# Attention with a bias on one core: late loads throttled by halves, new load times and due slots in the planner, 24 instead of 25 score tiles on VectorE

## The chip, the cores and the metric

The kernel runs on one core of a Trainium2 chip. The metric is the device time of one execution in microseconds. The profile shows one further execution, whose own time is given beside its span (first to last instruction).

## What is computed

```python
def reference(q, k, v, bias):            # q, k, v: (4, 8, 1024, 64) float32, bias: (1, 1, 1024, 1024)
    scale = 1.0 / np.sqrt(head_dim)
    scores = scale * np.matmul(q, k.transpose(0, 1, 3, 2)) + bias
    scores_max = np.max(scores, axis=-1, keepdims=True)
    attn = np.exp(scores - scores_max) / (np.sum(np.exp(scores - scores_max), axis=-1, keepdims=True) + 1e-8)
    return np.matmul(attn, v)
```

There are 32 heads of 1024 queries and 1024 keys, with 64 elements a head. The kernel leaves the maximum out and gets the sum of the exponentials from a column of ones beside V.

## The kernel before

**Slots.** The heads are taken as 16 pairs, and the queries of a head as 8 chunks of 128. One chunk of one head is a *slot*: a tile of 128 x 1024 scores. There are 256. The list `slots` holds them in order: two groups of pairs (7 and 9 pairs), and inside a group rounds that take several query chunks of each head in turn. Three places in PSUM (`places`, tile `pl`) hold the scores of three slots. The scores of a slot are made as a difference: the tile that the last slot left in its place is kept, and one product with doubled operands (`ko`/`qo` for an odd head, `ke`/`qe` for an even one) takes the last head's scores out and puts the new one's in. Only where a chain starts, the bias is written first, by a product with an identity (line 255).

**What happens to a slot.** TensorE fills the place (`fill`, line 258, eight matmuls). ScalarE then makes the exponentials of the whole tile in one instruction (`exp`, line 272) into one of 13 buffers `E`. For the slots in `PLAN`, VectorE makes them instead, in five steps (`d_steps`, lines 289, 294, 297, 300 and 305). TensorE multiplies the result with V and its column of ones (`av`, line 322, eight matmuls) into a bank `po` that takes six or seven slots. VectorE divides by the sums (`evac`, lines 350 and 352), and SyncE's queue stores the result.

**What comes before.** Of each pair, K and Q are loaded by GpSimd's DMA queue, which also turns float32 into bfloat16, into `land` tiles (`k16`, `q16`, five buffers each). TensorE transposes them in pieces (`transposes`, lines 195 and 199) into one of the two small PSUM buffers `xa` and `xb`, which the products with V share. VectorE copies them out to `ko` and `qo` (`copy_out`, lines 207 and 209). For the pairs from 7 on (`EARLY`), Q is then negated back into the tile that it was loaded into (`negate`, line 232), and SyncE's queue copies halves of `ko` and of the negated Q to `ke` and `qe` of this pair and of the next (`copy`, line 583). The loads of pairs 7 to 15 go in two halves each, one DMA a head: K and Q in `beside` (line 142), V straight into its place in `vall` (line 170).

**Who sets the order.** No loop runs over this. A planner in Python goes through the engines by estimated clocks (`t_pe`, `t_act`, `t_dve`, `t_pool`, `t_dma`) and writes out one program. Each engine works its instructions off in that order, and waits for what a tile's last user or writer has to do. The estimates decide only the order. The parts that matter here:

- `issue` (line 492) estimates when a load lands and holds loads back. The list `flight` holds each load's last element and its estimated landing. Before a load that would be too many, GpSimd copies one element of the load `depth` places back (`tick`, line 497), and so waits until that one has landed. `LATE` (3) is the depth for pairs 7 to 15, `DEEP` (4 and 5) that for the earlier loads.
- `COSTS` (2300 ns a load) is the estimated time of a late load, and `t_dma` the estimated end of the last one.
- `load` (line 503) issues K and Q of a pair as soon as the pair five back has freed its tiles, then queues V of the pair before; `next_v` issues V once its place in `vall` is free.
- `DUE` gives, for pairs 7 to 15, the slot by which a pair's transposes are due; a pair can be taken up to `AHEAD` (90) slots before. If it is due within 20 slots, its copies go first on VectorE.
- `PLAN` lists the slots whose exponentials VectorE makes.

The functions that the diff touches, and what calls them:

Of the kernel before, what the change touches and what calls it, by code (L numbers as in the profile page):

```python
# [16 lines left out]
def kernel(  # L17
# [79 lines left out]
    for g, n in enumerate(GROUPS):  # L97
        heads = list(range(2 * pr0, 2 * (pr0 + n)))
        rounds = []
        a = (len(heads) * 2 // 3 + 1) // 2 * 2  # L100
        tail = [(2, c, h, h == heads[a]) for c in (3, 4) for h in heads[a:]]
        assert len(tail) <= a
        middle = [[(0, 3, h, h == heads[0]), (1, 4, h, h == heads[0])] + tail[i:i + 1] for i, h in enumerate(heads[:a])]
        ends = [[[(x, c + x, h, h == heads[0] and (go or g == 0)) for x in range(3)] for h in heads]
                for go, c in enumerate((5, 0) if g % 2 else (0, 5))]
        rounds = ends[0] + middle + ends[1]
        first_pair.add(pr0)
        group_of[pr0] = g
# [14 lines left out]
    for s, x in enumerate(slots):  # L123
# [2 lines left out]


    dslots = set()
    PLAN = (42, 46, 54, 72, 74, 83, 90, 97, 107, 112, 135, 138, 151, 158, 161, 173, 180, 186, 194, 207, 213,
            217, 228, 238, 246)  # L130

    raws, lands, arrs = {}, {}, {}


    BESIDE, INPLACE = (0, 1), 7

    def beside(pr, x):

        raws[pr, x, 0] = t = land.tile([P, 2, NCH, D], BF, name="qk"[x] + "16").rearrange(
            "p t c d -> p (t c d)").rearrange("p (c t d) -> p c t d", t=2, d=D)  # L140
        for y in range(2):
            nc.gpsimd.dma_start(out=t[:, :, y, :], in_=(qf, kf)[x][pr][:, y].rearrange("p (c d) -> p c d", d=D))  # L142
        return t[:1, NCH - 1, 1, D - 1:]

    def load_k(pr):
        if pr >= EARLY and 1 in BESIDE:
            return beside(pr, 1)
        lands[pr, 1, 0] = t = land.tile([P, 2, NCH, D], BF, name="k16")
        nc.gpsimd.dma_start(out=t.rearrange("p t c d -> p t (c d)"), in_=kf[pr])
        return t[:1, 1, NCH - 1, D - 1:]  # L150

    def load_q(pr, cs):
        if pr >= EARLY and 0 in BESIDE:
            return beside(pr, 0)

        t = consts.tile([P, 2, NCH - C0, D], BF, name=f"qrest{pr}") if cs.start else land.tile([P, 2, NCH, D], BF, name="q16")
        lands[pr, 0, cs.start] = t
        to = t[:, :, :cs.stop - cs.start, :]
        nc.gpsimd.dma_start(out=to.rearrange("p t c d -> p t (c d)"),
                            in_=qf[pr][:, :, cs.start * D:cs.stop * D])  # L160
        return to[:1, 1, cs.stop - cs.start - 1, D - 1:]

    def load_b(c):
        nc.gpsimd.dma_start(out=braw[:, c, :], in_=bf_[:, c, :])
        return braw[:1, c, S - 1:]

    def load_v(pr):
        if pr >= INPLACE:
            for t in range(2):
                nc.gpsimd.dma_start(out=vall[:, (2 * pr + t) % VR, :, :D], in_=vf[pr][:, t])  # L170
            return vall[:1, (2 * pr + 1) % VR, NCH - 1, D - 1:D]
        lands[pr, "v"] = vland.tile([P, 2, NCH, D], BF, name="v16")
        nc.gpsimd.dma_start(out=lands[pr, "v"].rearrange("p t c d -> p t (c d)"),
                            in_=vf[pr].rearrange("p t c d -> p t (c d)"))
        return lands[pr, "v"][:1, 1, NCH - 1, D - 1:]

    def arrays(pr):
        if pr not in arrs:
# [176 lines left out]
    with tc.manual_schedule():  # L355
# [14 lines left out]

        nc.gpsimd.memset(qz[0][D:, :, :], 0.0)  # L371
        nc.gpsimd.memset(qs[D:, :, :], 0.0)  # L372
        for c in (1, 2):
            load_b(c)
        load_k(1)
        load_q(1, slice(0, C0))
        load_k(2)
        load_q(2, slice(0, NCH))
        load_v(0)
# [82 lines left out]
        free_lands, loads, loads_v = set(), list(range(EARLY, NP)), []  # L462
        sp_q, t_sp = [], T0
# [25 lines left out]
            while loads and loads[0] - LANDS in free_lands:  # L489
                load(loads.pop(0), t)  # L490

        def issue(at, cost, depth, load, pr, *a):

            nonlocal t_dma
            if 0 < depth <= len(flight):
                what, t = flight[-depth]
                nc.gpsimd.tensor_copy(tick[:], what)
                at = max(at, t + 100)
            two = pr >= EARLY and load in [load_q] * (0 in BESIDE) + [load_k] * (1 in BESIDE) or load is load_v and pr >= INPLACE
            at = pool(at, 1500 if two else 750)  # L500
            t_dma = max(t_dma + cost, at + 2200 + cost)
            flight.append((load(pr, *a), t_dma + 200))
            return t_dma + 200

        def load(pr, t):
            raw_at[pr, 1, 0] = issue(t, COSTS["k"], LATE, load_k, pr) + LATER
            raw_at[pr, 0, 0] = issue(t, COSTS["q"], LATE, load_q, pr, slice(0, NCH)) + LATER
            for p in [pr - 1] * (pr > EARLY) + [pr] * (pr + 1 == NP):
                loads_v.append(p)
            next_v(t)  # L510

        def next_v(t):

            while loads_v and not any(x[2] // 2 == loads_v[0] - VR // 2 and y not in av_done for y, x in enumerate(slots)):
                if loads_v[0] < INPLACE + VL and loads_v[0] - VL not in v_at:
                    break
                p = loads_v.pop(0)
                vland_at[p] = issue(t, COSTS["v"], LATE + (p > 12), load_v, p) + LATER
                move_v(p)

        def move_v(pr):
            if pr >= INPLACE:
                v_at[pr] = vland_at[pr] + 300
                return

            def run(t2):
                nc.vector.tensor_copy(vall[:, 2 * pr % VR:2 * pr % VR + 2, :, :D], lands[pr, "v"][:])
                v_at[pr] = t2 + 430 + L_DVE
                next_v(v_at[pr])
            dve_q.append((vland_at[pr] + VSLACK * (pr >= EARLY), 0.3, 430, run))  # L530

        def early(kind, pr):
            nonlocal t_dma
            late = kind + str(pr) in LATE_LOADS
            depth = DEEP[late]
            if kind == "k":
                raw_at[pr, 1, 0] = issue(0, E1, depth, load_k, pr) + SLACK
            elif kind == "q":
                cs = slice(0 if pr >= SPLIT else C0, NCH)
                raw_at[pr, 0, cs.start] = issue(0, E1 if pr >= SPLIT else E2, depth, load_q, pr, cs) + SLACK  # L540
                if late:
                    raw_at[pr, 0, cs.start] = LATE_LOADS["q%d" % pr]
            elif kind == "v":
                vland_at[pr] = issue(0, E1, depth, load_v, pr)
                if late:
                    vland_at[pr] = LATE_LOADS["v%d" % pr]
                move_v(pr)
            else:
                issue(0, E1, depth, load_b, pr)
                bias_at[pr] = LATE_LOADS["b%d" % pr]  # L550
            if late:
                t_dma = LATE_LOADS[kind + str(pr)] - 200
                flight[-1] = flight[-1][0], t_dma + 200

        def doubles(pr, which, c0, n, t2, urgent):
            if not which and pr >= EARLY:
# [63 lines left out]
        def sided(pr, which, c0):  # L620
            return SIDE <= pr < EARLY and c0 == 0
# [13 lines left out]
        def pe_cands():  # L635

            out = []
            for x in range(3):
# [4 lines left out]
                if r is not None and (before[s] is None or before[s] in used):  # L643
                    cost = FILL + BIAS * bool(slots[s][3] and s > 1)

                    def do(t, s=s, x=x, cost=cost):
                        nonlocal next_fill
                        fill(s)
                        filled[s] = t + cost + L_FILL
                        queue[x].pop(0)  # L650
                        next_fill = min([y[0] for y in queue.values() if y], default=NS)
                        if s in PLAN:
                            dslots.add(s)
                            avq.remove(s)
                            start_d(s)
                        else:
                            acts.append(s)
# [47 lines left out]
            if pieces:  # L705
# [5 lines left out]
                if (raw is not None and next_fill >= need - AHEAD and (ring < 0 or last_slot[ring] < next_fill)  # L711
                        and (lag < 7 or need - next_fill < 6)):
                    f, tag = min((x_free[y], y) for y in x_free)
                    r = max(f, raw)
                    cost = n * TR + SWITCH * (which not in BESIDE if pr >= EARLY else not sided(pr, which, c0))
# [205 lines left out]
```

## Time and profile before

| | |
|---|---|
| time, three runs | 230.83 us median (230.78 to 232.82) |
| the profiled execution | 232.22 us, span 230.4 us, granted clock 0.996 |
| busy: TensorE, ScalarE, VectorE, GpSimd | 219.2, 216.8, 204.0, 82.2 us |
| DMA moved | 29.74 MB, 129 GB/s on average |
| GpSimd's queue (loads) | 62880 packets, 14.06 MB |
| SyncE's and ScalarE's queue (copies, stores, first loads) | 28080 packets, 14.43 MB |

The profile gives busy time, idle time and its releaser for each group of instructions; the columns read "busy us, mean ns of one | idle us before it, and who ended that". Matmuls are pipelined, and their ends are modelled, so neighbouring rows overlap: the pace is read from start to start. A releaser "issue" means that the engine waited for nothing that the profile shows.

### The profile page before, as it was taken

To read this page: it belongs to the slowest core of one execution; us is meant where nothing else is said; L and a number is where in the kernel's file an instruction comes from. 1 tells how busy PE (TensorE), PEld (TensorE's weight loads), DVE (VectorE), ACT (ScalarE), POOL (GpSimd) and SP (SyncE) were. 2 spreads that over 40 slices of the span, in tenths; PEclk is the share of its full clock that TensorE was granted. 3 is DMA by queue.
4 is the path that set the end of the run, shared out by engine and by line. 5 is a ranking of instruction groups with operands and counts; after the bars stand their busy time and mean duration, and the time that the engine had idled before them with its cause. 6 is when DMAs were issued, how large, how long until landed. Compare 5 with 4: busy or idle time off the path is not lost.

```text
span 230.4 us, 10433 instructions
## 1 busy us (share of the span) xinstructions
PE 219.2 (95%) x4535; PEld 208.9 (91%) x4535; DVE 204.0 (89%) x304; ACT 216.8 (94%) x236; POOL 82.2 (36%) x133
## 2 busy tenths in 40 slices
PE   7899999999999999779999899999999999999993
PEld 2779989999999999779999899998999998999992
DVE  3487878679989999879999899999999999999994
ACT  4699999999999999789999899999999999999993
POOL 8826454599668696586246000000000000000000
PEclk9999999999999999999999999999999999999998
DMA  6999999999999999999979975102122111211313
GB/s 206 195 205 215 226 221 207 185 169 152 197 171 159 134 145 175 195 188 145 146 159 163 192 165 135 50 0 54 42 47 69 38 29 32 68 43 43 83 29 82
DMA packets 91437, 29.74 MB, mean 129 GB/s; under 512 B 74560, under 2 KB 87744, under 8 KB 91392
## 3 DMA queue, kind: packets, MB, share of 16 engines
q0 software_dynamic: 62880, 14.06, 67.7%
q1 hardware_dynamic: 28080, 14.43, 26.2%
q8 instruction: 35, 0.57, 1.1%
q10 hardware_dynamic: 432, 0.59, 1.0%
q14 instruction: 10, 0.08, 0.1%
HBM read 29.36 MB, written 8.39 MB: 164 GB/s over the span
## 4 chain that ended last, share of the span: by engine, by line
PE 59%; ACT 19%; issue 9%; DVE 6%; DMA 3%; POOL 1%; SPq 1%; POOLq 0%; ACTq 0%
PE pl L258 34%; ACT E L272 19%; PE po L322 18%; PE px L195 4%; DMA braw<-in_bias_dram 3%; PE pl L255 2%; DVE dy L289 2%; PE px L199 1%; DVE ob L352 1%; DMA out_dram<-ob 1%; DVE df L297 1%; SPq L757 1%; POOL qz L371 0%; POOL qs L372 0%; DVE ke L218 0%
## 5 line engine op out<-in xcount | busy, mean ns | idle before, releaser
L272 ACT ACTIVATE E<-pl 128x1024 bf16<-128x1024 f32 (+1 forms) x232 | 213.6, 1089 | 5.6 <-PE pl L258 5.5
L322 PE MATMUL po<-vall,E 128*128 128x65 bf16 x1848 | 87.5, 194 | 2.0 <-issue 1.2
L258 PE MATMUL pl<-qo,ko 128*128 128x128 bf16 x1024 | 76.5, 219 | 2.5 <-issue 1.5
L322 PEld LDWEIGHTS <-E 128*128 128x128 bf16 x1848 | 74.5, 98 | 2.9 <-issue 1.3
L258 PEld LDWEIGHTS <-ko 128*128 128x128 bf16 x1160 | 69.8, 98 | 5.2 <-issue 2.7
L258 PE MATMUL pl<-qe,ke 128*128 128x128 bf16 x888 | 65.9, 219 | 0.8 <-DVE dy L289 0.4
L258 PEld LDWEIGHTS <-ke 128*128 128x128 bf16 x888 | 53.2, 98 | 2.5 <-issue 1.0
L289 DVE TENSOR_SCALAR dy<-pl 128x1024 int32<-128x1024 f32 x25 | 30.5, 1219 | 3.2 <-PE pl L258 3.0
L305 DVE SCALAR_TENSOR_TENSOR de<-dy,df 128x1024 uint16<-128x1024 int32 x25 | 30.5, 1218 | 0.5 <-PE po L322 0.5
L297 DVE SCALAR_TENSOR_TENSOR df<-df 128x1024 f32<-128x1024 f32 x25 | 30.5, 1219 | 0.1
L300 DVE SCALAR_TENSOR_TENSOR df<-df 128x1024 f32<-128x1024 f32 x25 | 30.4, 1217 | 0.1
L352 DVE TENSOR_TENSOR ob<-po,rs 128x448 f32<-128x448 f32 (+5 forms) x41 | 23.5, 572 | 1.4
L142 POOL DMA_DIRECT2D q<-in_q_dram x18 | 15.9, 886 | 8.8 <-DVE ob L352 7.5
L294 DVE TENSOR_SCALAR df<-dy 128x1024 f32<-128x1024 uint16 x25 | 17.4, 701 | 0.1
L142 POOL DMA_DIRECT2D k<-in_k_dram x18 | 15.9, 888 | 2.9 <-PE px L195 2.0
L170 POOL DMA_DIRECT2D vall<-in_v_dram x18 | 15.8, 884 | 1.0 <-issue 0.9
L209 DVE TENSOR_SCALAR qo<-px,sgn 128x1024 bf16<-128x1024 bf16 (+2 forms) x18 | 12.3, 683 | 1.5 <-PE px L199 1.0
L207 DVE COPY ko<-px 128x1024 bf16<-128x1024 bf16 (+1 forms) x16 | 10.7, 669 | 3.2 <-PE px L199 2.6
L255 PE MATMUL pl<-ident,braw 128*128 128x128 bf16 x136 | 11.4, 227 | 0.2 <-DMA braw<-in_bias_dram 0.2
L350 DVE RECIPROCAL rs<-po 128x7 f32<-128x7 f32 (+5 forms) x42 | 8.1, 194 | 3.5 <-PE po L322 3.1
L322 PE MATMUL po<-vall,de 128*128 128x65 bf16 x200 | 10.5, 194 | 0.2 <-DVE ob L352 0.2
L255 PEld LDWEIGHTS <-braw 128*128 128x128 bf16 x136 | 10.0, 149 | 0.4 <-DMA braw<-in_bias_dram 0.3
(63 smaller groups left out, 124.3 us busy)
## 6 DMA issues: line engine op xcount, KB each, us to landing
out_dram<-ob SPq DMA_DIRECT2D x69, 64.0 KB, 1.8
ke<-ko SPq DMA_DIRECT2D x22, 128.0 KB, 5.5
out_dram<-ob SPq DMA_DIRECT2D x27, 96.0 KB, 4.7
k<-in_k_dram POOLq DMA_DIRECT2D x18, 128.0 KB, 5.9
q<-in_q_dram POOLq DMA_DIRECT2D x18, 128.0 KB, 6.7
vall<-in_v_dram POOLq DMA_DIRECT2D x18, 128.0 KB, 6.0
qe<-q SPq DMA_DIRECT2D x17, 128.0 KB, 5.5
braw<-in_bias_dram POOLq DMA_DIRECT2D x7, 256.0 KB, 5.6
```

The costliest lines, as they stand in the source:

```text
L142: nc.gpsimd.dma_start(out=t[:, :, y, :], in_=(qf, kf)[x][pr][:, y].rearrange("p (c d) -> p c d", d=D))
L170: nc.gpsimd.dma_start(out=vall[:, (2 * pr + t) % VR, :, :D], in_=vf[pr][:, t])
L255: nc.tensor.matmul(to, braw[:, c, :].rearrange("p (kp kc) -> p kc kp", kc=NCH)[:, kc, :], ident8[:], start=i == 0, stop=False, skip_group_ ...
L258: nc.tensor.matmul(to, kk[:, kc, :], qq[:, c, :], start=False, stop=True, skip_group_check=True)
L272: nc.scalar.activation(e[:, i:i + n].rearrange("p b x -> p (b x)"), places[slots[s][0]][:, i:i + n].rearrange("p b x -> p (b x)"), ACTF.Ex ...
L289: w.tensor_scalar(t["y"][:], places[slots[s][0]].rearrange("p b x -> p (b x)"), scale * LOG2E * 65536.0, 127.0 * 65536.0, op0=ALU.mult, op ...
L294: w.tensor_scalar(t["f"][:], t["lo"], GU / 65536.0, None, op0=ALU.mult)
L297: w.scalar_tensor_tensor(t["f"][:], t["f"][:], GP, t["f"][:], op0=ALU.add, op1=ALU.mult)
L300: w.scalar_tensor_tensor(t["f"][:], t["f"][:], GQ, t["f"][:], op0=ALU.add, op1=ALU.mult)
L305: w.scalar_tensor_tensor(etile[s].bitcast(U16).rearrange("p c q -> p (c q)"), t["y"][:], 1.0 / 512.0, t["f"][:], op0=ALU.mult, op1=ALU.add)
L322: nc.tensor.matmul(po[:, j + i, :], etile[s][:, kc, :], vall[:, slots[s][2] % VR, kc, :], start=j + i + kc == 0, stop=kc == NCH - 1, skip_ ...
L352: nc.vector.tensor_tensor(ob[:, :n, :], po[:, :n, :D], rs[:, :n, :].to_broadcast([P, n, D]), op=ALU.mult)
```

## The change

The throttle now counts each half of a late load by itself, with an estimated time of its own. Before a DMA is issued, the estimated times of the ones before it are added up from the latest back, as long as the sum with its own stays within `back`; GpSimd then waits, by a tick, for the last one outside. For pairs 7 to 15 `back` is 5900 ns, and a load in halves counts 2900 ns, so four halves may be under way; a load in one piece would count 1650 ns. For the earlier loads `back` is four or five times 1450 ns, which leaves their ticks as they were. The model's time of a late load becomes 2900 ns in place of 2300. `DUE` and `PLAN` have new values; `PLAN` has 24 slots in place of 25. `BESIDE` and `INPLACE` become ranges that name the same pairs as before, the loading functions return their DMAs as a list that `issue` works off, and the new formula for `a` gives the same values for both groups.

```diff
-        a = (len(heads) * 2 // 3 + 1) // 2 * 2
+        a = -(-len(heads) // 3) * 2
...
-    PLAN = (42, 46, 54, 72, 74, 83, 90, 97, 107, 112, 135, 138, 151, 158, 161, 173, 180, 186, 194, 207, 213,
-            217, 228, 238, 246)
+    PLAN = (41, 42, 47, 56, 76, 79, 88, 110, 120, 132, 137, 143, 154, 162, 170, 178, 188, 193, 207, 211, 220,
+            224, 234, 246)
...
-    BESIDE, INPLACE = (0, 1), 7
+    BESIDE = {0: range(7, 16), 1: range(7, 16)}
+    INPLACE = range(7, 16)
...
-        for y in range(2):
+
+        def piece(y):
             nc.gpsimd.dma_start(out=t[:, :, y, :], in_=(qf, kf)[x][pr][:, y].rearrange("p (c d) -> p c d", d=D))
-        return t[:1, NCH - 1, 1, D - 1:]
+            return t[:1, NCH - 1, y, D - 1:]
+        return [lambda y=y: piece(y) for y in range(2)]
...
-        DUE = (56, 89, 71, 156, 50, 70, 141, 54, 56)
+        DUE = (62, 165, 107, 90, 92, 50, 117, 128, 110)
...
-        LATE, COSTS = 3, {"k": 2300, "q": 2300, "v": 2300}
+        BACK, SPREAD, WHOLE = 5900, 2900, 1650
...
-        DEEP = {True: 4, False: 5}
+        DEEP = {True: 4 * 1450, False: 5 * 1450}
...
-        def issue(at, cost, depth, load, pr, *a):
+        def issue(at, cost, back, load, pr, *a):
             nonlocal t_dma
-            if 0 < depth <= len(flight):
-                what, t = flight[-depth]
-                nc.gpsimd.tensor_copy(tick[:], what)
-                at = max(at, t + 100)
-            two = pr >= EARLY and load in [load_q] * (0 in BESIDE) + [load_k] * (1 in BESIDE) or load is load_v and pr >= INPLACE
-            at = pool(at, 1500 if two else 750)
-            t_dma = max(t_dma + cost, at + 2200 + cost)
-            flight.append((load(pr, *a), t_dma + 200))
+            jobs = load(pr, *a)
+            for do in jobs:
+                part = cost / len(jobs)
+                behind, j = part, len(flight)
+                while j and behind + flight[j - 1][2] <= back:
+                    j -= 1
+                    behind += flight[j][2]
+                if j:
+                    nc.gpsimd.tensor_copy(tick[:], flight[j - 1][0])
+                    at = max(at, flight[j - 1][1] + 100)
+                at = pool(at, 750)
+                t_dma = max(t_dma + part, at + 2200 + part)
+                flight.append((do(), t_dma + 200, part))
             return t_dma + 200
...
-            raw_at[pr, 1, 0] = issue(t, COSTS["k"], LATE, load_k, pr) + LATER
-            raw_at[pr, 0, 0] = issue(t, COSTS["q"], LATE, load_q, pr, slice(0, NCH)) + LATER
+            raw_at[pr, 1, 0] = issue(t, SPREAD if pr in BESIDE[1] else WHOLE, BACK, load_k, pr) + LATER
+            raw_at[pr, 0, 0] = issue(t, SPREAD if pr in BESIDE[0] else WHOLE, BACK, load_q, pr, slice(0, NCH)) + LATER
...
-                vland_at[p] = issue(t, COSTS["v"], LATE + (p > 12), load_v, p) + LATER
+                vland_at[p] = issue(t, SPREAD if p in INPLACE else WHOLE, BACK, load_v, p) + LATER
```

More of the change, by code (lines that the diff above doesn't have):

```diff
@@ L140, in beside @@
             "p t c d -> p (t c d)").rearrange("p (c t d) -> p c t d", t=2, d=D)
-        for y in range(2):
+        def piece(y):
             nc.gpsimd.dma_start(out=t[:, :, y, :], in_=(qf, kf)[x][pr][:, y].rearrange("p (c d) -> p c d", d=D))
-        return t[:1, NCH - 1, 1, D - 1:]
+            return t[:1, NCH - 1, y, D - 1:]
+        return [lambda y=y: piece(y) for y in range(2)]
     def load_k(pr):
-        if pr >= EARLY and 1 in BESIDE:
+        if pr in BESIDE[1]:
             return beside(pr, 1)
-        lands[pr, 1, 0] = t = land.tile([P, 2, NCH, D], BF, name="k16")
@@ L149, in load_k, with piece @@
-        nc.gpsimd.dma_start(out=t.rearrange("p t c d -> p t (c d)"), in_=kf[pr])
-        return t[:1, 1, NCH - 1, D - 1:]
+        def piece():
+            lands[pr, 1, 0] = t = land.tile([P, 2, NCH, D], BF, name="k16")
+            nc.gpsimd.dma_start(out=t.rearrange("p t c d -> p t (c d)"), in_=kf[pr])
+            return t[:1, 1, NCH - 1, D - 1:]
+        return [piece]
     def load_q(pr, cs):
-        if pr >= EARLY and 0 in BESIDE:
+        if pr in BESIDE[0]:
             return beside(pr, 0)
-        t = consts.tile([P, 2, NCH - C0, D], BF, name=f"qrest{pr}") if cs.start else land.tile([P, 2, NCH, D], BF, name="q16")
@@ L157, in load_q, with piece @@
[L157 to L161, printed above, removed]
+        def piece():
+            t = consts.tile([P, 2, NCH - C0, D], BF, name=f"qrest{pr}") if cs.start else land.tile([P, 2, NCH, D], BF, name="q16")
+            lands[pr, 0, cs.start] = t
+            to = t[:, :, :cs.stop - cs.start, :]
+            nc.gpsimd.dma_start(out=to.rearrange("p t c d -> p t (c d)"),
+                                in_=qf[pr][:, :, cs.start * D:cs.stop * D])
+            return to[:1, 1, cs.stop - cs.start - 1, D - 1:]
@@ L163, in load_b, with piece @@
+        return [piece]
     def load_b(c):
-        nc.gpsimd.dma_start(out=braw[:, c, :], in_=bf_[:, c, :])
-        return braw[:1, c, S - 1:]
+        def piece():
+            nc.gpsimd.dma_start(out=braw[:, c, :], in_=bf_[:, c, :])
+            return braw[:1, c, S - 1:]
+        return [piece]
     def load_v(pr):
[L168 to L175, printed above, removed]
+        def rows():
+            lands[pr, "v"] = vland.tile([P, 2, NCH, D], BF, name="v16")
+            nc.gpsimd.dma_start(out=lands[pr, "v"].rearrange("p t c d -> p t (c d)"),
+                                in_=vf[pr].rearrange("p t c d -> p t (c d)"))
+            return lands[pr, "v"][:1, 1, NCH - 1, D - 1:]
@@ L177, in arrays, with piece @@
+        def piece(t):
+            nc.gpsimd.dma_start(out=vall[:, (2 * pr + t) % VR, :, :D], in_=vf[pr][:, t])
+            return vall[:1, (2 * pr + t) % VR, NCH - 1, D - 1:D]
+        return [lambda t=t: piece(t) for t in range(2)] if pr in INPLACE else [rows]
     def arrays(pr):
@@ L372 @@
         nc.gpsimd.memset(qs[D:, :, :], 0.0)
[L373 to L379, printed above, removed]
+        for do in load_b(1) + load_b(2) + load_k(1) + load_q(1, slice(0, C0)) + load_k(2) + load_q(2, slice(0, NCH)) + load_v(0):
+            do()
         for i in range(10):
@@ L514, in next_v @@
             while loads_v and not any(x[2] // 2 == loads_v[0] - VR // 2 and y not in av_done for y, x in enumerate(slots)):
-                if loads_v[0] < INPLACE + VL and loads_v[0] - VL not in v_at:
+                if loads_v[0] not in INPLACE and loads_v[0] - VL not in v_at:
                     break
                 p = loads_v.pop(0)
-                vland_at[p] = issue(t, COSTS["v"], LATE + (p > 12), load_v, p) + LATER
+                vland_at[p] = issue(t, SPREAD if p in INPLACE else WHOLE, BACK, load_v, p) + LATER
                 move_v(p)
         def move_v(pr):
-            if pr >= INPLACE:
+            if pr in INPLACE:
                 v_at[pr] = vland_at[pr] + 300
@@ L552, in early @@
                 t_dma = LATE_LOADS[kind + str(pr)] - 200
-                flight[-1] = flight[-1][0], t_dma + 200
+                flight[-1] = flight[-1][0], t_dma + 200, flight[-1][2]
         def doubles(pr, which, c0, n, t2, urgent):
@@ L714, in pe_cands @@
                     r = max(f, raw)
-                    cost = n * TR + SWITCH * (which not in BESIDE if pr >= EARLY else not sided(pr, which, c0))
+                    cost = n * TR + SWITCH * (pr not in BESIDE[which] if pr >= EARLY else not sided(pr, which, c0))
                     urgent = need - next_fill < 20
```

## The prediction

> **What bounds the kernel now.** I read the page first, for who is busy; then ScalarE's timeline, for where the busiest engine pauses; then TensorE's timeline at those pauses.
>
> ```profile
> span 230.4 us, 10433 instructions
> ...
> PE 219.2 (95%) x4535; PEld 208.9 (91%) x4535; DVE 204.0 (89%) x304; ACT 216.8 (94%) x236; POOL 82.2 (36%) x133
> ```
>
> Three engines are near full, so the page alone names no bound. ScalarE's timeline does (start, length, instructions merged; the bracket is idle time before the row, and who ended it):
>
> ```profile
> 10.87 36.82 ACT L272 ACTIVATE E<-pl 128x1024 bf16<-128x1024 f32 x40 [0.27 <-PE pl L258]
> 48.13 10.25 ACT L272 ACTIVATE E<-pl 128x1024 bf16<-128x1024 f32 x11 [0.44 <-PE pl L258]
> 58.72 13.03 ACT L272 ACTIVATE E<-pl 128x1024 bf16<-128x1024 f32 x14 [0.34 <-PE pl L258]
> 72.09 21.48 ACT L272 ACTIVATE E<-pl 128x1024 bf16<-128x1024 f32 x23 [0.34 <-PE pl L258]
> 94.18 1.94 ACT L272 ACTIVATE E<-pl 128x1024 bf16<-128x1024 f32 x2 [0.61 <-PE pl L258]
> 96.81 4.69 ACT L272 ACTIVATE E<-pl 128x1024 bf16<-128x1024 f32 x5 [0.69 <-PE pl L258]
> 101.79 1.02 ACT L272 ACTIVATE E<-pl 128x1024 bf16<-128x1024 f32 x1 [0.28 <-PE pl L258]
> 103.39 28.52 ACT L272 ACTIVATE E<-pl 128x1024 bf16<-128x1024 f32 x31 [0.58 <-PE pl L258]
> 132.52 61.65 ACT L272 ACTIVATE E<-pl 128x1024 bf16<-128x1024 f32 x67 [0.61 <-PE pl L258]
> 194.35 32.19 ACT L272 ACTIVATE E<-pl 128x1024 bf16<-128x1024 f32 x35 [0.17 <-PE pl L258]
> ```
>
> From 10.87 us to the end ScalarE runs one exponential after another, with nine pauses. The difference of two unbroken runs gives the price of one: (61.65 - 28.52) / (67 - 31) = 0.92 us. So ScalarE sets the end, and any gain must come out of the pauses. They sum to 4.06 us: 1.12 at 48 to 72 us, 2.77 in the five from 94.18 to 132.52, and 0.17 late. Each is put down to a fill of scores by TensorE that came late. What made TensorE late at the five large ones stands in its own timeline:
>
> ```profile
> 91.52 0.42 PE L322 MATMUL po<-vall,E 128*128 128x65 bf16 x8
> 91.79 0.33 PE L258 MATMUL pl<-qo,ko 128*128 128x128 bf16 x3
> 93.64 0.44 PE L258 MATMUL pl<-qo,ko 128*128 128x128 bf16 x5 [1.52 <-issue]
> ...
> 99.25 0.26 PE L322 MATMUL po<-vall,E 128*128 128x65 bf16 x3
> 100.66 0.41 PE L322 MATMUL po<-vall,E 128*128 128x65 bf16 x8 [1.16 <-issue]
> ...
> 130.58 0.33 PE L195 MATMUL px<-ident,q 128*128 128x128 bf16 x3
> 131.59 0.45 PE L195 MATMUL px<-ident,q 128*128 128x128 bf16 x5 [0.68 <-issue]
> 131.88 0.61 PE L258 MATMUL pl<-qe,ke 128*128 128x128 bf16 x8
> 132.32 0.61 PE L258 MATMUL pl<-qo,ko 128*128 128x128 bf16 x8
> ```
>
> Three times TensorE stands still in the middle of eight equal matmuls (three done, five to go), for 1.52, 1.16 and 0.68 us, and the trace names no semaphore. Data cannot be what is missing there, since the same operands were just in use. I take it that the instructions themselves came late:
>
> ```profile
> q8 instruction: 35, 0.57, 1.1%
> ```
>
> 0.57 MB in 35 packets is 16 KB a packet; TensorE's 2 x 4535 recorded instructions over 35 are 259 a packet. These packets use the DMA engines that the loads fill:
>
> ```profile
> 50.00:60.00 10.00, 10.00 (x214) 9.88 (x212) 9.67 (x14) 9.66 (x12) 9.00 (x14) 1.00 1.94 161
> 140.00:150.00 10.00, 9.92 (x220) 9.62 (x217) 9.23 (x12) 10.00 (x12) 0.00 (x0) 1.00 0.39 93
> ```
>
> (The last three columns of these windows are granted clock, DMA share and GB/s.) The DMA share is 1.94 while loads run and 0.39 once they are over, and no such stall is left after 132 us.
>
> **The change part by part.** *One VectorE slot fewer.* One of 256 score tiles goes from VectorE to ScalarE: +0.92 us on the engine that sets the end, and nothing hides it. VectorE is freed of one chain of five steps:
>
> ```profile
> L289 DVE TENSOR_SCALAR dy<-pl 128x1024 int32<-128x1024 f32 x25 | 30.5, 1219 | 3.2 <-PE pl L258 3.0
> L305 DVE SCALAR_TENSOR_TENSOR de<-dy,df 128x1024 uint16<-128x1024 int32 x25 | 30.5, 1218 | 0.5 <-PE po L322 0.5
> L297 DVE SCALAR_TENSOR_TENSOR df<-df 128x1024 f32<-128x1024 f32 x25 | 30.5, 1219 | 0.1
> L300 DVE SCALAR_TENSOR_TENSOR df<-df 128x1024 f32<-128x1024 f32 x25 | 30.4, 1217 | 0.1
> L352 DVE TENSOR_TENSOR ob<-po,rs 128x448 f32<-128x448 f32 (+5 forms) x41 | 23.5, 572 | 1.4
> L294 DVE TENSOR_SCALAR df<-dy 128x1024 f32<-128x1024 uint16 x25 | 17.4, 701 | 0.1
> L209 DVE TENSOR_SCALAR qo<-px,sgn 128x1024 bf16<-128x1024 bf16 (+2 forms) x18 | 12.3, 683 | 1.5 <-PE px L199 1.0
> L207 DVE COPY ko<-px 128x1024 bf16<-128x1024 bf16 (+1 forms) x16 | 10.7, 669 | 3.2 <-PE px L199 2.6
> ...
> L232 DVE TENSOR_SCALAR q<-qo 128x1024 bf16<-128x1024 bf16 x9 | 4.2, 472 | 0.8
> ```
>
> 1.219 + 0.701 + 1.219 + 1.217 + 1.218 = 5.57 us. VectorE isn't the bound, so this is worth only what pauses it causes: at most the 1.12 + 0.17 us outside the five. By the order of the built programs the stretch of fills 37 to 79 keeps its transposes and biases and has six VectorE slots, not five, so I take -0.2, with bounds -1.29 and 0.
>
> *Two loads' worth under way.* The late loads of pairs 7 to 15 are 54 halves of 128 KB. Now a pair of halves waits for the load three back; afterwards every half waits for the half four back, with a tick of its own (27 more ticks). GpSimd's timeline gives the pace:
>
> ```profile
> 44.95 1.77 POOL L142 DMA_DIRECT2D k<-in_k_dram  x2 [0.28 <-PE pl L258]
> ...
> 50.86 0.18 POOL L497 COPY tick<-k 1x1 bf16<-1x1 bf16 x1
> 51.29 1.74 POOL L142 DMA_DIRECT2D q<-in_q_dram  x2 [0.25 <-issue]
> ...
> 85.58 1.74 POOL L170 DMA_DIRECT2D vall<-in_v_dram  x2 [0.28 <-issue]
> ```
>
> Sixteen loads (K7 to Q12, V7 to V10) are issued between the first and the last row: 40.63 / 32 = 1.27 us a half. Afterwards a half costs GpSimd 1.74 / 2 + 0.18 + 0.25 = 1.30 us before any wait, so I take 1.4. The 17 loads up to V11 are then issued by 45 + 34 x 1.4 = 92.6 us and landed some 6 us later. Behind a waiting tick stand only loads: GpSimd does nothing else by then. The next user is TensorE, which in the new order transposes K8 after fill 103. Counting ScalarE's rows, about 98 exponentials and 8 VectorE slots are done at 103.4 us, so this is near 100 us: all has landed. K13 to V15 (20 halves) wait for buffers that pairs 8 to 10 free, so they run from some 108 to 136 us; Q15, the tightest, lands near 132 us and is transposed after fill 147, near 139. Cost 0; with one 2.5 us load later than that, up to +1.
>
> [...]
>
> *What this does to instruction blocks.* Fewer load packets queue ahead of each block. Also the copies of doubled K and Q on SyncE's queue, some of which now fall at 82 to 92 us, beside the loads, move to fills 103 to 116, when few loads run. Landing times of such copies (minimum, median, maximum) at 82 to 92.5 us and at 109 to 119 us:
>
> ```profile
> DMA to landing us min/median/max: 4.9/6.7/7.3
> ...
> DMA to landing us min/median/max: 2.2/3.2/4.2
> ```
>
> With loads a copy takes 6.7 us, without them 3.2. A queue of four halves for six should cut such delays by a third or more: of the three stalls I let 0.9 us of the 2.77 stay, -1.8. Bounds: all of it (-2.77), or one more stall of the first kind (+0.61 + 0.69 = +1.3), since loads and copies still meet after 110 us.
>
> *Moved transposes.* Pairs 8 to 12 are now transposed back to back: ten pieces between fills 103 and 116, where before pairs 8 and 9 came at fills 83 to 92 and the others apart. VectorE must copy each out and negate Q: 5 x (0.669 + 0.683 + 0.472) = 9.1 us, plus one eviction (0.572) and a first step for slot 110 (1.219): 10.9 us. ScalarE needs 12 x 0.92 = 11.0 us for the same stretch, TensorE 13 x 0.44 for fills and as much for ten pieces at about that price: 10.1 us; it postpones all products with V for ten fills. There is no room, but no overload either. Price 0 to +2.0 (the eviction and the first step, 1.8, entirely in the way, and some waits); by the nearest row, the same work spread at 113 to 130 us with no pause in 28.5 us, I take +0.5.
>
> **Sum.** 0.92 - 0.2 + 0 - 1.8 + 0.5 = -0.58 us. The profiled execution took 232.22 us (span 230.4 and 1.8 around it), which gives 231.6; it lies 1.39 above the median 230.83 of runs between 230.78 and 232.82. Against the median: 230.3 us.
>
> **The rivals.** (1) *No relief.* The stalls stay: the limit only just bites (1.30 us of GpSimd work against 1.27 us), the DMA engines stay as full, and the exponential is paid: 230.83 + 0.92 = 231.75, with the +0.5 232.2. For it: DMA share 1.94 comes from the bytes to be moved, which don't change. Against: landing times do follow the queue. [...]
>
> (2) *Faster by over 1%.* All five pauses go, and most of the others: 230.83 + 0.92 - 2.77 - 0.9 = 228.1. For it: VectorE gets 5.57 us, and loads and copies are parted. Against: the rows at 48 to 72 us, where TensorE has biases and transposes to do in either order.
>
> (3) *Slower by over 1%.* The ten pieces cost the full +2.0: VectorE falls behind, a transpose finds both its buffers taken, TensorE's postponed products with V use up the 13 buffers of exponentials, and ScalarE waits; the stalls stay too, with twenty copies in that stretch: 230.83 + 0.92 + 2.0 = 233.75. It decides once pauses grow by 1.4 us in all (2.3 less 0.92). For it: 10.9 us of VectorE against 11.0. Against: the 28.5 us without a pause.
>
> **How the numbers follow.** Forecast 0.40, rival 1 0.15, rival 2 0.25, rival 3 0.20. A measurement of this kernel tells about 1% (2.3 us) from no change; so faster 0.25, within it 0.55, slower 0.20. The range goes from nearly all pauses gone (230.83 + 0.92 - 4.06 = 227.7, taken as 227.8) to just short of rival 3's full price, 233.4; the forecast and rival 1 alone span 229 to 232.3.
>
> **What would show it.** Right: 231 whole exponentials on ScalarE (with the two halves of the first, 233 rows), 24 first steps of 1.2 us on VectorE, idle before fills from 80 to 135 us near 1 us, no load waited for by TensorE, ticks waiting on halves. Wrong: mid-group stalls on TensorE as long as now; a pause over 0.5 us on ScalarE near fills 103 to 120, put down to VectorE's copies; or a transpose that waits for a landing.

## The result, and the profile after

| | median of 20 | lowest to highest | ratio to before (95%) |
|---|---|---|---|
| before | 230.81 us | 228.44 to 232.82 | |
| after | 233.38 us | 231.28 to 236.64 | 1.0112 (1.0084 to 1.0139) |

The change makes the kernel 1.1% slower, 2.6 us; 0.2% faster was forecast. The profiled execution of after took 232.55 us (span 230.8), 0.8 under its median, while that of before lay 1.4 above its own: the pauses read below differ in size from one execution to the next, so verdicts go by the ratios, and the traces tell the places. The kernel's lines stand 2 to 15 further down (the fills at 270, the exponentials at 284, the late loads at 144 and 185, the ticks at 510).

The page of after, busy time of each engine:

```profile
span 230.8 us, 10486 instructions
...
PE 218.8 (95%) x4535; PEld 208.9 (91%) x4535; DVE 200.0 (87%) x299; ACT 216.7 (94%) x237; POOL 95.5 (41%) x160
```

ScalarE's timeline of after:

```profile
9.39 37.46 ACT L284 ACTIVATE E<-pl 128x512 bf16<-128x512 f32 x41 [0.56 <-PE pl L270]
48.13 23.94 ACT L284 ACTIVATE E<-pl 128x1024 bf16<-128x1024 f32 x26 [1.28 <-PE pl L270]
72.41 50.55 ACT L284 ACTIVATE E<-pl 128x1024 bf16<-128x1024 f32 x55 [0.33 <-PE pl L270]
124.88 11.11 ACT L284 ACTIVATE E<-pl 128x1024 bf16<-128x1024 f32 x12 [1.93 <-PE pl L270]
137.21 89.94 ACT L284 ACTIVATE E<-pl 128x1024 bf16<-128x1024 f32 x98 [1.22 <-PE pl L270]
```

The five pauses of before from 94 to 132 us are gone, and so are the small ones at 58.72 and 194.35 us. Three large ones stand instead: 1.28 us at 48 us (0.44 before), 1.93 us at 125 and 1.22 us at 137 us. TensorE's timeline of after at the two last:

```profile
120.29 0.61 PE L270 MATMUL pl<-qo,ko 128*128 128x128 bf16 x8
123.08 0.61 PE L207 MATMUL px<-ident,k 128*128 128x128 bf16 x8 [2.18 <-issue]
...
134.39 0.61 PE L270 MATMUL pl<-qe,ke 128*128 128x128 bf16 x8
136.12 0.61 PE L207 MATMUL px<-ident,q 128*128 128x128 bf16 x8 [1.11 <-DMA q<-in_q_dram]
```

These stalls are of another kind than those of before: the group of eight ahead is whole, and the next work is a transpose of a tile that is being loaded, K of pair 14 and Q of pair 15. For the first the view names no semaphore, so I looked at GpSimd's timeline of after for that load (two DMAs, at 111.90 and 115.15), and at the landing times of these two:

```profile
100.30 0.18 POOL L510 COPY tick<-vall 1x1 bf16<-1x1 bf16 x1 [0.84 <-DMA vall<-in_v_dram]
106.83 0.87 POOL L144 DMA_DIRECT2D q<-in_q_dram  x1 [6.36 <-PE px L207]
...
111.90 0.88 POOL L144 DMA_DIRECT2D k<-in_k_dram  x1
114.41 0.68 POOL L510 COPY tick<-q 1x1 bf16<-1x1 bf16 x1 [1.63 <-DMA q<-in_q_dram]
115.15 0.98 POOL L144 DMA_DIRECT2D k<-in_k_dram  x1
...
DMA to landing us min/median/max: 7.8/7.8/7.8
```

115.15 + 7.8 = 123.0 us, and TensorE goes on at 123.08. So GpSimd held the second half of K14 until an earlier half had landed, and that half took 7.8 us. Before that it stood idle for 6.36 us for the Q tile of pair 8. The row names the transposes, which were long done (by 99.42 us); the last to use that tile are copies of its negated Q. SyncE's copies from 97 to 116 us (the third value is the range of their starts), and their landing times:

```profile
L595 SPq DMA_DIRECT2D ke<-ko x10: 467/541/908, 97.4 to 112.3; - x10
L595 SPq DMA_DIRECT2D qe<-q x10: 461/589/1038, 101.2 to 114.3; - x10
...
DMA to landing us min/median/max: 3.2/4.7/7.2
```

The first two copies of a negated Q start at 101.24 and 101.8 us and take 4.5 to 4.7 us to land, so the last is there by some 106.5 us; GpSimd goes on at 106.83. In all K14 goes out 15 us later than before (its first half at 111.90 in place of 96.95 us): 7.9 us because the loads ahead of it went at the slower pace (K13 at 97.60 in place of 89.73), and most of the rest by this wait of 6.36.

### The profile page after: what moved, and what is told of

Read it like the earlier page. It is cut to its first block, busy times and chain, and to the rows that moved or that the text cites. A ratio compares the mean times of both kernels' runs of the same rounds, so it can differ in the third digit from the quotient of the medians.

```text
span 230.8 us, 10486 instructions
## 1 busy us (share of the span) xinstructions
PE 218.8 (95%) x4535; PEld 208.9 (91%) x4535; DVE 200.0 (87%) x299; ACT 216.7 (94%) x237; POOL 95.5 (41%) x160
## 4 chain that ended last, share of the span: by engine, by line
PE 49%; ACT 26%; issue 13%; DMA 6%; DVE 3%; POOL 1%; ACTq 0%; POOLq 0%
PE pl L270 29%; ACT E L284 26%; PE po L334 14%; PE px L207 3%; DMA q<-in_q_dram 2%; DMA braw<-in_bias_dram 2%; PE pl L267 2%; DMA ke<-ko 2%; DVE ko L219 1%; PE px L211 1%; DVE side L238 0%; POOL qz L383 0%; DVE ke L230 0%; POOL qs L384 0%; DVE qo L221 0%
## 5 line engine op out<-in xcount | busy, mean ns | idle before, releaser
L301 DVE TENSOR_SCALAR dy<-pl 128x1024 int32<-128x1024 f32 x24 | 29.3, 1219 | 4.7 <-PE pl L270 4.3
L317 DVE SCALAR_TENSOR_TENSOR de<-dy,df 128x1024 uint16<-128x1024 int32 x24 | 29.1, 1218 | 0.2
L309 DVE SCALAR_TENSOR_TENSOR df<-df 128x1024 f32<-128x1024 f32 x24 | 29.1, 1218 | 0.1
L312 DVE SCALAR_TENSOR_TENSOR df<-df 128x1024 f32<-128x1024 f32 x24 | 29.1, 1218 | 0.1
L364 DVE TENSOR_TENSOR ob<-po,rs 128x448 f32<-128x448 f32 (+4 forms) x41 | 23.5, 572 | 1.5
L144 POOL DMA_DIRECT2D k<-in_k_dram x18 | 17.3, 961 | 2.3 <-issue 2.1
L510 POOL COPY tick<-k 1x1 bf16<-1x1 bf16 x22 | 9.3, 421 | 8.8 <-DMA k<-in_k_dram 8.6
L362 DVE RECIPROCAL rs<-po 128x7 f32<-128x7 f32 (+4 forms) x42 | 8.1, 193 | 3.9 <-PE po L334 3.5
```

What stands on the lines that cost most here:

```text
L301: w.tensor_scalar(t["y"][:], places[slots[s][0]].rearrange("p b x -> p (b x)"), scale * LOG2E * 65536.0, 127.0 * 65536.0, op0=ALU.mult, op ...
L309: w.scalar_tensor_tensor(t["f"][:], t["f"][:], GP, t["f"][:], op0=ALU.add, op1=ALU.mult)
L312: w.scalar_tensor_tensor(t["f"][:], t["f"][:], GQ, t["f"][:], op0=ALU.add, op1=ALU.mult)
L317: w.scalar_tensor_tensor(etile[s].bitcast(U16).rearrange("p c q -> p (c q)"), t["y"][:], 1.0 / 512.0, t["f"][:], op0=ALU.mult, op1=ALU.add)
L364: nc.vector.tensor_tensor(ob[:, :n, :], po[:, :n, :D], rs[:, :n, :].to_broadcast([P, n, D]), op=ALU.mult)
```

## The experiments

Theory 1: the throttle slows the loads, and those of pairs 13 to 15 land too late. Theory 2: the new due slots do it, because the late transposes of pairs 8 to 10 keep the tiles that these loads need. Theory 3: the loss is the slot moved to ScalarE, with the bunched slots 41 and 42. Ratios are to the kernel before, timed beside each run on the same chip.

**Six halves under way in the changed kernel** (`a_ticks6`).

```diff
-                    nc.gpsimd.tensor_copy(tick[:], flight[j - 1][0])
+                    jj = j - 2 * (back == BACK)
+                    nc.gpsimd.tensor_copy(tick[:], flight[jj - 1][0])
```

> The changed kernel with every late tick two halves further back (six halves under way, as before), the planner's arithmetic and so the order on all engines untouched. Theory 1 (the throttle makes the loads of pairs 13 to 15 late, a half takes 1.6 us where it took 1.3): the two pauses of ScalarE at 125 and 137 us (1.9 and 1.2 us) go, some 230.5 us, with mid-group stalls of TensorE perhaps back. Theory 2 (the new due slots: K13 to V15 start only near 107 us, whatever the depth): the pauses stay, within 1 us of the changed kernel. Theory 3 (the slot moved to ScalarE and the bunched first slots 41, 42, 47): no change, 233.4 us.

Measured: 234.27 us, ratio 1.0190 (1.0144 to 1.0236): slower, not faster. No transpose waits for a landing any more, but TensorE's timeline has the stalls inside groups back:

```profile
116.28 0.35 PE L334 MATMUL po<-vall,E 128*128 128x65 bf16 x6
118.28 0.23 PE L334 MATMUL po<-vall,E 128*128 128x65 bf16 x2 [1.65 <-issue]
...
123.98 0.29 PE L334 MATMUL po<-vall,de 128*128 128x65 bf16 x4
125.85 0.29 PE L334 MATMUL po<-vall,de 128*128 128x65 bf16 x4 [1.58 <-issue]
...
131.36 0.33 PE L270 MATMUL pl<-qo,ko 128*128 128x128 bf16 x3
133.49 0.45 PE L270 MATMUL pl<-qo,ko 128*128 128x128 bf16 x5 [1.79 <-issue]
```

5.0 us of them. That instructions are what comes late here I read from the DMA view, cut into short windows. Its queue 8 moves packets of instructions; the view names no engine for them, and I take them for TensorE's, which runs 9070 of the 10433 recorded instructions of before. These packets start at 115.7, 123.2 and 130.9 us, each 7.4 to 7.7 us behind the one before, and each of the three stalls ends 2.6 us after such a start. So in this order either depth loses: four halves wait for landings, six, by this reading, for instructions.

**The parts by themselves.** Six runs mix old and new throttle, due slots and VectorE slots. Where due slots, VectorE slots or load times differ, the planner writes another order, so these tell what a part costs in its company, not a term to be added.

```diff
 a_due_old (after)       -DUE = (62, 165, 107, 90, 92, 50, 117, 128, 110)   +DUE = (56, 89, 71, 156, 50, 70, 141, 54, 56)
 a_plan_old (after)      -PLAN = (41, 42, 47, ...)  24 slots                +PLAN = (42, 46, 54, ...)  25 slots
 a_due_plan_old (after)  both of these
 b_due_new (before)      +DUE = (62, 165, 107, 90, 92, 50, 117, 128, 110)
 b_plan_new (before)     +PLAN = (41, 42, 47, ...)  24 slots
 b_halves4 (before)      one tick for each half, on the half four back; planner and order untouched
```

> The changed kernel with the due slots of before. Theory 1: the pace of 1.6 us a half stays, so half of the lateness stays: about 232 us. Theory 2: pairs 8 and 9 give their buffers back 15 us earlier, no transpose waits for a landing, 230 to 230.5 us. Theory 3: 233 us.

> The changed kernel with the 25 VectorE slots of before. Theories 1 and 2: one exponential fewer and no more, about 232.5 us. Theory 3: also the pause of 1.3 us at 48 us falls to 0.4, 231.6 us.

> The kernel before with a tick for every half of a late load and four halves under way, its planner and so the order on all other engines untouched. Theory 1: the last loads land later, 1 to 3 us slower than before (232 to 234 us). Theories 2 and 3: not slower; with fewer mid-group stalls of TensorE 0 to 2 us faster (229 to 231 us).

> The changed kernel with both the due slots and the 25 VectorE slots of before: the throttle by halves and the new load times alone. If these two cost nothing by themselves (four halves under way were no slower than six in the old order): the time of the kernel before, ratio 0.995 to 1.005. If the new load times make a worse order: 1.01 or more.

> The kernel before with the due slots of after alone. Theory 2 (late transposes of pairs 8 to 10 hold back the loads of pairs 13 to 15): slower by 1 to 2 us, ratio 1.005 to 1.009, with pauses of ScalarE between 115 and 140 us. Theories 1 and 3: ratio 1.000.

> The kernel before with the 24 VectorE slots of after alone. One exponential more (0.9 us) and the pause at 48 us as in the changed kernel (1.3 in place of 0.4): 1.8 us slower, ratio 1.008, if the new order loses nothing else; with late landings as in the other mixtures 1.012 or more.

| throttle | due slots | VectorE slots | run | us | ratio (95%) |
|---|---|---|---|---|---|
| halves, old order | old | old | b_halves4 | 229.76 | 1.0003 (0.9980 to 1.0026) |
| halves, new load times | old | old | a_due_plan_old | 232.85 | 1.0126 (1.0084 to 1.0168) |
| old | new | old | b_due_new | 236.24 | 1.0269 (1.0229 to 1.0309) |
| old | old | new | b_plan_new | 231.61 | 1.0074 (1.0044 to 1.0104) |
| new | old | new | a_due_old | 231.58 | 1.0074 (1.0045 to 1.0103) |
| new | new | old | a_plan_old | 236.28 | 1.0273 (1.0235 to 1.0310) |

Theory 1 fails as stated: in the old order the throttle costs nothing. The new due slots cost most, 2.7%, with six halves under way (`b_due_new`), at least three times what was expected of them. The changed kernel with the old VectorE slots (`a_plan_old`) loses as much, where every theory had it a little faster than the changed kernel. TensorE's timeline of `b_due_new`, and the landing times of the halves of K and Q issued from 112 to 121 us:

```profile
123.57 0.61 PE L258 MATMUL pl<-qo,ko 128*128 128x128 bf16 x8
126.14 0.61 PE L195 MATMUL px<-ident,k 128*128 128x128 bf16 x8 [1.96 <-issue]
...
127.99 0.61 PE L258 MATMUL pl<-qe,ke 128*128 128x128 bf16 x8
129.80 0.61 PE L195 MATMUL px<-ident,q 128*128 128x128 bf16 x8 [1.20 <-DMA q<-in_q_dram]
...
DMA to landing us min/median/max: 9.6/10.7/12.2
```

The same wait, without the throttle: theory 2. In `a_plan_old` too TensorE waits 2.69 us before the transposes of a K tile. ScalarE's pauses from 125 to 136 us in `b_due_new` sum to 3.9 us of the 6.2 lost; where the rest goes is not shown. The new load times give another order, which loses 1.3%; TensorE's timeline of that run (`a_due_plan_old`) has stalls inside groups, the largest this:

```profile
121.90 0.83 PE L270 MATMUL pl<-qe,ke 128*128 128x128 bf16 x12
124.35 0.38 PE L270 MATMUL pl<-qe,ke 128*128 128x128 bf16 x4 [1.62 <-issue]
```

With the old due slots the changed kernel loses 0.7%, where it lost 1.1 (the intervals overlap). With the new VectorE slots alone the kernel before loses the same 0.7%, 1.7 us. The exponential (0.92) and the longer pause at 48 us (0.84) make 1.76, as theory 3 has it; but the trace doesn't show that this is the whole account, as in the same execution the two pauses of 0.34 us at 58 and 72 us are gone and others of 0.41 to 0.62 us stand from 129 to 137 us. ScalarE's timeline of this last run (`b_plan_new`) at that pause:

```profile
48.20 40.72 ACT L272 ACTIVATE E<-pl 128x1024 bf16<-128x1024 f32 x44 [1.28 <-PE pl L258]
```

**The late landings taken away** (`a_v_last`): the changed kernel, with four halves of V moved behind the loads of K and Q on GpSimd's queue, and nothing else moved.

```diff
+                hold = load is load_v and pr in (12, 13)
...
+                if hold:
+                    held.append(do)
...
+                while held and load is load_q and pr + 1 == NP and do is jobs[-1]:
+                    nc.gpsimd.tensor_copy(tick[:], hist[-4])
+                    hist.append(held.pop(0)())
```

> The changed kernel with the four halves of V of pairs 12 and 13 issued after Q of pair 15, still four halves under way; the order of all other engines untouched. K14, Q14, K15 and Q15 then land 3 to 6 us earlier. Theories 1 and 2 (these landings are what the pauses at 125 and 137 us wait for): both pauses go, 1.5 to 3 us faster than the changed kernel, ratio to before 1.000 to 1.005. Theory 3: no change, 1.011.

Measured: 229.44 us, ratio 0.9988 (0.9959 to 1.0018), against 1.0112 for the changed kernel. ScalarE's timeline:

```profile
48.09 23.94 ACT L284 ACTIVATE E<-pl 128x1024 bf16<-128x1024 f32 x26 [1.28 <-PE pl L270]
72.37 151.38 ACT L284 ACTIVATE E<-pl 128x1024 bf16<-128x1024 f32 x165 [0.33 <-PE pl L270]
```

165 exponentials without a pause. The two pauses of 1.93 and 1.22 us were 3.15 us of the profiled execution, and 1.24%, 2.9 us, come back. This settles the place: the last loads of K and Q land too late.

**Why they land so late** (`a_small_copies`): the changed kernel with 12 copies cut to an eighth. What they would have filled is left out: the even heads of pairs 10 to 12 use the odd heads' operands.

```diff
-        return (t["ko"], t["qo"]) if h % 2 else (t["ke"], t["qe"])
+        return (t["ko"], t["qo"]) if h % 2 or 10 <= pr <= 12 else (t["ke"], t["qe"])
...
+            if 10 <= pr + (x == 1) <= 12:
+                nc.sync.dma_start(out=arrays(pr + (x == 1))[name][rows, :1, :], in_=source[rows, :1, :])
```

> The changed kernel with 12 of the 20 copies of doubled K and Q at fills 103 to 116 cut to an eighth (those into the even operands of pairs 10 to 12; the even heads of these pairs use the odd heads' operands instead, so their scores are left wrong); the order of all engines untouched. If the copies slow the loads: halves issued at 108 to 120 us land in 5 to 6 us in place of 7 to 8, the two pauses shrink by 1.5 us or more together, ratio to before 1.003 or less. If the loads are slow by themselves: same landings, ratio 1.011.

Measured: 229.84 us, ratio 0.9992 (0.9957 to 1.0028). The landing times of K14 and of Q14's first half, issued from 109.5 to 112.6 us, and ScalarE's timeline:

```profile
DMA to landing us min/median/max: 5.9/6.0/6.6
...
72.46 151.39 ACT L284 ACTIVATE E<-pl 128x1024 bf16<-128x1024 f32 x165 [0.33 <-PE pl L270]
```

With 12 copies cut, the halves of K14 land in 6.6 and 5.9 us, not 7.8. As the loads ahead land sooner too, the second half goes out at 111.6 us, not 115.15, and is there 5.4 us earlier. The wait for the Q tile of pair 8 stays (6.37 us), and both pauses are gone, at the same depth and with GpSimd's order untouched. So the copies that the new due slots pack into fills 103 to 116 take the loads' time.

**How many halves should be under way** (`av_ticks6`, `av_ticks3`: V last, six and three, here against `a_v_last`; `b_halves3`: the kernel before, three).

```diff
-                        nc.gpsimd.tensor_copy(tick[:], hist[-4])
+                        nc.gpsimd.tensor_copy(tick[:], hist[-6])
```

> V of pairs 12 and 13 after Q of pair 15, but six halves under way; order of the other engines untouched. If the throttle keeps the instruction blocks in time: mid-group stalls of TensorE come back, 1.5 to 4 us slower than with four halves, ratio to before 1.005 to 1.016. If the throttle has no such effect: the same time as with four, ratio 0.999.

> V of pairs 12 and 13 last, with three halves under way. If the blocks' lateness follows the number under way and loads still land in time: 0 to 0.5 us faster than with four, ratio 0.997 to 0.999. If three are too few for the loads: K14 or K15 is waited for, ratio over 1.005.

> The kernel before with three halves under way, order of the other engines untouched. If the blocks' lateness follows the number under way: faster than with four (which was equal to before), ratio 0.992 to 0.998. If it is chance of phase: 1.000; if three are too few for the loads: over 1.005.

Measured: 234.65 us, ratio 1.0217 (1.0174 to 1.0260) with six; 235.90, 1.0211 (1.0149 to 1.0274) with three; 240.37, 1.0424 (1.0371 to 1.0478) with three in the old order. TensorE's timelines, six, then three, then three in the old order:

```profile
128.71 0.33 PE L270 MATMUL pl<-qo,ko 128*128 128x128 bf16 x3
132.21 0.45 PE L270 MATMUL pl<-qo,ko 128*128 128x128 bf16 x5 [3.17 <-issue]
...
112.19 0.61 PE L270 MATMUL pl<-qo,ko 128*128 128x128 bf16 x8
117.81 0.48 PE L207 MATMUL px<-ident,k 128*128 128x128 bf16 x3 [5.02 <-issue]
...
129.64 0.61 PE L270 MATMUL pl<-qo,ko 128*128 128x128 bf16 x8
138.88 0.58 PE L207 MATMUL px<-ident,k 128*128 128x128 bf16 x4 [8.62 <-DMA k<-in_k_dram]
```

With six, a stall inside a group; with three, whole groups and then a wait for a landing: in `av_ticks3` the second half of that K tile goes out at 110.41 us and takes 7.3 us, and TensorE goes on at 117.81. Of these three depths four is the best in the order with V last, 2.2% under either; five was not run.

**The bunched slots** (`a_first4`, `av_first4`, `av_slot44`).

```diff
-    PLAN = (41, 42, 47, 56, 76, ...
+    PLAN = (42, 46, 54, 66, 76, ...      # a_first4; av_first4 with V last
+    PLAN = (41, 44, 47, 56, 76, ...      # av_slot44, with V last
```

> The changed kernel with VectorE's first four slots at 42, 46, 54 and 66 in place of 41, 42, 47 and 56; still 24, and the transposes keep their places within one fill. Theory 3 (the bunched slots 41, 42 make the pause of 1.3 us at 48 us): the pause falls to 0.4 us, 0.8 us faster than the changed kernel, ratio to before 1.007 to 1.008. Theories 1 and 2: no change, 1.011.

> Both edits together: V of pairs 12 and 13 after Q of pair 15, and VectorE's first four slots at 42, 46, 54 and 66. If the late landings were the whole loss of the run with those slots alone: no pause over 0.5 us is left, 0.8 us faster than with V last alone, ratio to before 0.995. If the order with these slots loses elsewhere too: 1.000 or more.

> V of pairs 12 and 13 last, as in the run that did this alone, and VectorE's second slot at 44 in place of 42; the order of TensorE is that run's again from fill 80 on, and GpSimd's is the same throughout. If the slots 41 and 42 back to back make the pause of 1.3 us at 48 us: it falls to 0.4 us or less, and the run is 0.8 us faster than with V last alone, 228.6 us, ratio to before 0.995. If that pause is TensorE's own work (bias and transposes at that place): it stays, ratio 0.999.

Measured: 237.54 us, 1.0277 (1.0216 to 1.0338); 231.63, 1.0061 (1.0027 to 1.0095); 230.45, 1.0004 (0.9974 to 1.0034). The pause at 48 us shrinks in all three, but none is faster than before. ScalarE's timelines of `a_first4`, then of `av_slot44`:

```profile
47.86 10.24 ACT L284 ACTIVATE E<-pl 128x1024 bf16<-128x1024 f32 x11 [0.42 <-PE pl L270]
...
125.86 1.02 ACT L284 ACTIVATE E<-pl 128x1024 bf16<-128x1024 f32 x1 [3.70 <-PE pl L270]
...
46.88 1.98 ACT L284 ACTIVATE E<-pl 128x1024 bf16<-128x1024 f32 x2 [0.33 <-PE pl L270]
49.23 1.94 ACT L284 ACTIVATE E<-pl 128x1024 bf16<-128x1024 f32 x2 [0.38 <-PE pl L270]
51.34 20.41 ACT L284 ACTIVATE E<-pl 128x1024 bf16<-128x1024 f32 x22 [0.18 <-PE pl L270]
...
118.70 4.69 ACT L284 ACTIVATE E<-pl 128x1024 bf16<-128x1024 f32 x5 [0.64 <-PE pl L270]
```

In `a_first4` 1.28 becomes 0.42, and the pause behind the wait for K14 grows to 3.70 us. With V last that wait goes (1.0061 for 1.0277), but that run (`av_first4`) is 0.7% slower than V last alone, where 0.8 us faster was expected: a stall of 1.04 us inside a group stands at 123 us. In `av_slot44` 1.28 becomes 0.33 + 0.38 + 0.18 = 0.89, and pauses behind stalls inside groups come back from 118.70 us on, though TensorE's order from fill 80 and GpSimd's order are those of `a_v_last`. (The profiled execution lay 1.0 us above its run's median, that of `a_v_last` 0.2 below, so a typical one may hold less of them.) Why those stalls come in the one and not in the other stays open.

None of the 15 versions is clearly faster than the kernel before; the best, V last, ties with it and is 1.2% under the changed kernel.

## Why the prediction was wrong, step by step

*What bounds the kernel:* right. ScalarE sets the end, and the larger losses above show as pauses of its timeline.

*One slot fewer, +0.92:* borne out; 0.92 and the pause at 48 us fit the loss of the new VectorE slots alone. *The other slots, -0.2, bounds -1.29 and 0:* wrong in sign. I counted the slots of the stretch and didn't look at their neighbours: at 41 and 42 VectorE holds two of the three places at once (its first steps run from 45.78 to 48.42 us), and the pause grew by 0.84 us. With the small pauses that went (0.34 at 58.72 us, 0.17 late) and 0.01 at 72 us, 1.29 became 1.61: +0.3 in all. A loss should have been inside the bounds.

*Two loads' worth under way, 0, at most +1:* this is the step that failed. Its pace was 1.4 us a half; the first 34 halves (42.66 to 96.61 us) took 1.63 each. It followed Q15 alone as the tightest, to land near 132 us; it landed at 136.0, and K14, which I had not followed, 2.2 us after TensorE wanted it. And it put the fills at the times of before, stalls included: Q15 was to be wanted near 139 us, and TensorE wanted it at 135.0. The cost is 2.9 us by the run with V last, where at most 1 was allowed. The depth alone was not at fault (`b_halves4`, 1.0003): it needed the due slots, which delayed these loads by a further 6.36 us and put twenty copies beside them, and which bring the same wait with six halves under way (`b_due_new`). I had counted those copies as parted from the loads; they met the next ones.

*Instruction blocks, -1.8, bounds -2.77 and +1.3:* right that the stalls would go: the profile of after shows all 2.77 gone. But 2.77 was read from an execution 1.4 us above its median, and taken off the median. What the terms leave over, as an estimate, is 2.6 - 0.92 - 0.3 - 2.9 = -1.5 us, so the forecast of -1.8 was near, though not for the reason given (0.9 of 2.77 left). With V last four halves are 2.2% under six. But in the old order four are worth nothing, and why is not shown: the one trace of `b_halves4` is of an execution 3.4 us above its run's median. There too TensorE has a stall inside a group:

```profile
122.05 0.50 PE L270 MATMUL pl<-qe,ke 128*128 128x128 bf16 x6
124.77 0.40 PE L270 MATMUL pl<-qe,ke 128*128 128x128 bf16 x2 [2.22 <-issue]
```

That the missing thing is instructions is my reading of the packets of queue 8. The DMA view of before from 81.1 to 92.1 us has

```profile
q8 instruction: 1, 0.02, 1.0%
```

One packet in 11 us, where, as an estimate (9070 instructions in 35 packets, 259 each), the 214 matmuls and 212 weight loads from 50 to 60 us use up one in 6.1; this one starts at 90.3, and the stall ended at 93.64. From 45 to 220 us, 8 of the 17 profiled kernels have stalls of over 0.4 us inside a group, 17 in all, of 0.5 to 3.2 us, and each of them ends 2.2 to 3.4 us after the start of such a packet. Not every late packet stalls TensorE: with V last one starts 8.4 us behind the one before, and no group is torn. That the packets are late because of the loads beside them is not shown so directly; it rests on the runs with six halves. Nor do four halves rule the stalls out: `av_first4` and `av_slot44` have them at that depth. How far the depth itself keeps the blocks in time, and how far the accident of an order, stays open.

*Moved transposes, +0.5:* the direct price was 0: from 72.41 us on, 55 exponentials run without a pause through the whole cluster. Rival 3 named the right side, and its 233.75 us lies near the measured 233.38, but by luck: of its mechanism nothing shows, neither a pause in the cluster nor stalls that stay. The cluster cost through its copies' DMA time, which I had not priced: with twelve of them cut the ratio is 0.9992 in place of 1.0112. None of my rivals was a late landing, though I listed it among the signs of being wrong.

## What to carry to other kernels

When a throttle, an order and a set of due times change together, follow every transfer of the last batch to its user, not only the last one, and with the times that hold once the stalls you expect to remove are gone. A move that is free on the engines can still cost DMA time (here 1.2% came back with twelve copies cut): price the copies that it packs together against the loads beside them. And where the user of a late transfer can't move, what is queued ahead of it and not yet wanted can: four halves of V put behind K and Q gave back the whole loss (0.9988 in place of 1.0112). And a sum taken off a median should start from pauses of a typical execution: one that lies 1.4 us above it may have pauses that a typical one has not.

## What was not expected of the hardware

In the order with V last, four halves under way beat both neighbours that were run: three starve the transposes (a wait of 5.0 us), six cost up to 3.2 us at once in stalls inside groups, and either costs some 2% against four. In the old order six and four are level, and three cost 4% (a wait of 8.6 us). And the landing time of a 128 KB half moves with what runs beside it at the same depth: 7.8 us beside twenty copies, 5.9 to 6.6 with twelve of them cut.
